# Heads of the first phase: queries and keys written from PSUM into the attention's operand tiles, without the way through DRAM

## The chip, the cores and the metric

The kernel runs on one core of a Trainium2 chip. The metric is the device time of one execution in microseconds (us). Three runs of the kernel before took 1397.95, 1398.54 and 1400.02 us; their median, 1398.54 us, is the time before. The profile is of one further execution. Its engines are PE (TensorE's matmuls; PEld is its weight loads), DVE (VectorE), ACT (ScalarE), POOL (GpSimd) and SP, whose queue issues nearly all DMAs.

## The reference

One layer of a hybrid encoder, run on 1024 prompt frames and on 32 sample frames of a running stream. The part that matters here is the input projection and the forgetting attention ("fox", 8 heads of 64) of the prompt:

```python
h = x * (1 + sc1) + sh1                      # x: 1056 x 1024 in all, sc1/sh1 from the conditioning vector
mq, mk, mv, mo, mi, mf, fq, fk, fv, ff, gu, gv = split(h @ w_in)
logf = log_sigmoid(ff + b_fox_f)             # a forget value for each frame and head
Ft = cumsum(logf)                            # over the frames
# in blocks of 128 queries:
logits = q @ k.T * 64 ** -0.5 + F[query] - F[key], masked causally
out = softmax(logits) @ v
```

Beside it stand an mLSTM (4 heads, with its own gates `mi`, `mf` and a running maximum over the frames), a gated spatial unit, the output projection with a norm, and a SwiGLU feed-forward with a norm. The keys `fk` are also an output of their own.

## The kernel before, in words

**Tiles and phases.** The frames are cut in two groups: group 0 is frames 0 to 511, group 1 is frames 512 to 1023 and the 32 sample frames. A float32 product is made as three matmuls on split operands (high by high, high by low, low by high; `gemm`, L111). The modulated input lies in SBUF as `h1h` and `h1l`. `fm_unit` (L236) makes 128 output columns of the projection: it loads and splits the weights (`weights`, L94: ACT writes the high part, DVE or POOL the low part), then runs one gemm for each range of frames, of 256 frames in group 0 and 272 in group 1, each into a PSUM bank of pool `pg`, which has three. `tm_unit` (L272) does the same with the frames on the partitions.

The first phase works on group 0. The string `ORDER` (L42) is its list of work: `q0` to `q7` are the units of fox head 0 to 7 (64 columns of queries and 64 of keys in one unit), `f0` to `f7` the attention of each head over the first 512 frames, `k0`, `k1`, `v`, `o` the mLSTM's projections, `m0` to `m3` its chunks, `a` a piece of the conditioning. Heads 0 and 1 (`QD`) run their group 1 ranges in the same unit; the other heads' come later.

**A head's way to its operands.** For each range `evac_qk` (L359) writes the high part `qkh` (ACT, L366, with the scale 0.125 on the query rows), the low part `qkl` (DVE, L367) and their sum `qkr` (POOL, L368), and stores them to DRAM: `dqh`, `dql`, and the output `o_kT`. `fox` (L672) then loads nine pieces into five tiles: `qp` (queries high over low), `k1` (keys high, twice), `q2` (queries high and four rows of forget terms), `k2` (keys low and four rows), `v`. `fox_chunk` (L699) makes the scores with two matmuls for each block of 128 queries (L717, L718), the mask, maximum, exponential and sum, the transposes of the probabilities (L753) and the product with `v` (L761 to L770).

**The gates.** `gates` (L387) comes ahead of `ORDER`. From the 16 gate columns it makes, mostly on DVE and on few partitions, the forget sums, which it stores as `dfs` in eight pieces (L434 to L442, tile `gates_fr` with two buffers), the running maximum of the mLSTM (`gates_cm`, seven doubling steps on DVE at L454 with small copies on POOL at L455), the values `gates_rs` (L484 to L487), and nine PE transposes of these (L492) into `col`. Its tiles lie in a pool of their own that is closed at the end of the function. The pool `mx0` (L1316), from which the operand tiles of fox and the tiles of the mLSTM come, is opened after that, and takes up the space again; a tile there waits until what lay in its place has been used.

**What sets the order.** A planner arranges the instructions of each engine when the kernel is built, by its own estimate of when each is ready; attention and mLSTM carry a higher priority (`HPA`, L1341). On the chip each engine, and SP's queue, then works through its list strictly in that order.

Of the kernel before, what the change touches and what calls it, by code (L numbers as in the profile page):

```python
# [7 lines left out]
F32 = mybir.dt.float32  # L8
F32R = mybir.dt.float32r
AF = mybir.ActivationFunctionType  # L10
ALU = mybir.AluOpType
# [54 lines left out]
def f(ap):  # L66
    return ap.bitcast(F32)


class Kernel:  # L70
# [288 lines left out]
    def evac_qk(self, h):  # L359
        nc = self.nc  # L360

        def evac(o, n, ps):
            hi = self.t(self.sm, [P, 272], F32R, "qkh", 3)
            lo = self.t(self.sm, [P, 272], F32R, "qkl", 2)
            kr = self.t(self.sm, [P, 272], F32, "qkr", 3)
            nc.scalar.activation(hi[:, :n], ps, AF.Copy, scale=self.qsc)  # L366
            nc.vector.scalar_tensor_tensor(lo[:, :n], ps, self.qsc, f(hi[:, :n]), ALU.mult, ALU.subtract)  # L367
            nc.gpsimd.tensor_tensor(kr[:, :n], f(hi[:, :n]), f(lo[:, :n]), ALU.add)  # L368
            self.store(self.dqh[h, :, o:o + n], f(hi[:, :n]))
            self.store(self.dql[h, :, o:o + n], f(lo[:, :n]))  # L370
            self.store(self.d["o_kT"][h, :, o:o + n], kr[64:, :n])
            if o + n == T:
                nc.gpsimd.tensor_copy(self.qks[:, h, :], kr[:, n - NS:n])
        return evac

    def evac_mqk(self, i, scale):
        nc = self.nc

        def evac(o, n, ps):
            r = self.t(self.sm, [P, 272], F32, "qkr", 3)  # L380
            nc.scalar.activation(r[:, :n], ps, AF.Copy, scale=scale)
            self.store(self.dmqk[:, i, o:o + n], r[:, :n])
        return evac
# [288 lines left out]
    def fox(self, h, chunks):  # L672
        self.phase = "fox"
        mx = self.mx
        q0, q1 = chunks[0][0] * P, (chunks[-1][-1] + 1) * P
        nq, nk, nb = q1 - q0, q1, q1 // P
        t = lambda shape, dt, tag, bufs: self.t(mx, shape, dt, tag, bufs)
        b = self.foxbufs
        k1 = t([P, nk], F32R, "k1", b[0])
        qp = t([P, nq], F32R, "qp", b[1])  # L680
        k2 = t([68, nk], F32R, "k2", b[2])
        q2 = t([68, nq], F32R, "q2", b[1])
        v = t([P, nb, P], F32R, "v", b[3])
        qs = slice(q0, q1)
        self.load(f(qp[0:64]), self.dqh[h, 0:64, qs])
        self.load(f(qp[64:128]), self.dql[h, 0:64, qs])
        self.load(f(k1[0:64]), self.dqh[h, 64:128, :nk])
        self.load(f(k1[64:128]), self.dqh[h, 64:128, :nk])
        self.load(f(q2[0:64]), self.dqh[h, 0:64, qs])
        self.load(f(q2[64:68]), self.dfs[h, 2:6, qs])  # L690
        self.load(f(k2[0:64]), self.dql[h, 64:128, :nk])
        self.load(f(k2[64:68]), self.dfs[h, 0:4, :nk])
        self.load(f(v), self.dv[:, :nb, h * P:(h + 1) * P])
        for tiles in chunks:
            o = tiles[0] * P - q0
            n = len(tiles) * P
            yield from self.fox_chunk(h, tiles, nk, n, k1, k2, qp[:, o:o + n], q2[:, o:o + n], v)

    def fox_chunk(self, h, tiles, W, nq, k1, k2, qp, q2, v):  # L699
        nc, mx = self.nc, self.mx  # L700
        nb = tiles[-1] + 1
        t = lambda shape, dt, tag, bufs: self.t(mx, shape, dt, tag, bufs)
        b5 = self.foxbufs[4]
        probs = []
        for i in tiles:
            n = (i + 1) * P
            qc = slice((i - tiles[0]) * P, (i - tiles[0] + 1) * P)
            half = n if n <= 512 else (n // 2 + 127) // 128 * 128
            cuts = [(0, half)] + ([(half, n)] if half < n else [])
            mxs = self.t(mx, [P, 2], F32, "fmx", 3)  # L710
            sums = self.t(mx, [P, 2], F32, "fsm", 3)
            pr = t([P, W], F32, "p", 4)
            banks = []
            for x, (lo, hi) in enumerate(cuts):
                s = self.t(self.pss, [P, 512], F32, "s")
                w = hi - lo
                nc.tensor.matmul(s[:, :w], qp[:, qc], k1[:, lo:hi], start=True, stop=False)  # L717
                nc.tensor.matmul(s[:, :w], q2[:, qc], k2[:, lo:hi], start=False, stop=True)  # L718
                if hi == n:
                    nc.vector.tensor_tensor(s[:, w - P:w], s[:, w - P:w], self.maskneg, ALU.add)  # L720
                nc.vector.tensor_reduce(mxs[:, x:x + 1], s[:, :w], AX.X, ALU.max, negate=True)
                banks.append(s)
            if len(cuts) > 1:
                nc.vector.tensor_tensor(mxs[:, 0:1], mxs[:, 0:1], mxs[:, 1:2], ALU.min)  # L724
            for x, (lo, hi) in enumerate(cuts):
                nc.scalar.activation(pr[:, lo:hi], banks[x][:, :hi - lo], AF.Exp, bias=mxs[:, 0:1],  # L726
                                     accum_out=sums[:, x:x + 1])
            if len(cuts) > 1:
                nc.vector.tensor_tensor(sums[:, 0:1], sums[:, 0:1], sums[:, 1:2], ALU.add)
            nc.vector.reciprocal(sums[:, 0:1], sums[:, 0:1])  # L730
            if FP[tiles[0] // 4]:
                nc.scalar.activation(pr[:, :n], pr[:, :n], AF.Copy, scale=sums[:, 0:1])
            else:
                nc.vector.tensor_scalar(pr[:, :n], pr[:, :n], sums[:, 0:1], None, ALU.mult)
            probs.append(pr)
            yield
            self.phase = "fox"


        o = self.t(self.po, [P, 512], F32, "o")  # L740
        full = tiles[0] + 1
        order = [0] + list(range(full, nb)) + list(range(1, full))
        units = [order[x:x + 2] for x in range(0, nb, 2)] if full > 1 else [[0], [1], [2, 3]]
        held = None
        for unit in units:
            ps = self.t(self.pt, [P, 512], F32, "t")
            at, e = [], 0
            for b in unit:
                first = max(0, b - tiles[0])
                w = nq - first * P  # L750
                for y in range(first, len(tiles)):
                    c = e + (y - first) * P
                    nc.tensor.transpose(ps[:, c:c + P], probs[y][:, b * P:(b + 1) * P], self.ident)  # L753
                at.append((b, slice(e, e + w), slice(first * P, nq)))
                e += w
            ph = t([P, 512], F32R, "pth", b5)
            pl = t([P, 512], F32R, "ptl", 2)
            nc.scalar.copy(ph[:, :e], ps[:, :e])
            nc.vector.tensor_tensor(pl[:, :e], ps[:, :e], f(ph[:, :e]), ALU.subtract)
            for b, c, q in at:  # L760
                nc.tensor.matmul(o[:, q] if b == 0 else o[0:64, q], v[:, b, :] if b == 0 else v[:, b, 0:64],  # L761
                                 pl[:, c], start=b == 0, stop=False)
                if b == 0 and full == 1:
                    held = ph
                else:
                    nc.tensor.matmul(o[:, q], v[:, b, :], ph[:, c], start=False, stop=full > 1 and b == order[-1])
            yield
            self.phase = "fox"
        if held is not None:
            nc.tensor.matmul(o[:, :nq], v[:, 0, :], held[:, :nq], start=False, stop=True)  # L770
        tmp = t([64, nq], F32, "fo", 1)
        r = t([64, nq], F32, "fr", 1)
        nc.scalar.copy(tmp[:, :nq], o[64:128, :nq])
        nc.vector.tensor_tensor(r[:, :nq], o[0:64, :nq], tmp[:, :nq], ALU.add)
        c = tiles[0] // 4
        o = tiles[0] * P - GO[c]
        self.store(self.dmix[c][64 * (h % 2):64 * (h % 2) + 64, 2 + h // 2, o:o + nq], r[:, :nq])
# [467 lines left out]
    def run(self):  # L1245
# [68 lines left out]
        more(T1[3])  # L1314
        s2 = ExitStack()
        self.mx = self.pool("mx0", ctx=s2)  # L1316
        self.foxbufs = (2, 1, 1, 2, 3)

        def emit(x):
            eng = nc.gpsimd if x[-1] == "p" else nc.vector  # L1320
# [4 lines left out]
            if x[0] == "m":  # L1325
                return self.mlstm(i)
            if x[0] == "q":
                self.fm_unit(w3[2 + i], self.evac_qk(i), (0, 1) if i < QD else (0,), eng)
            elif x[0] == "k":
                self.fm_unit(w3[i], self.evac_mqk(2 + i, 0.125), eng=eng)  # L1330
            elif x[0] == "s":
                self.mlstm_states()
            elif x[0] == "a":
                more(1)
            else:
                self.tm_unit(w2["-vo".index(x)], 256, self.evac_raw((None, self.dmv, self.dmo)["-vo".index(x)]), eng=eng)
# [251 lines left out]
```

## Time and profile before

| | |
|---|---|
| median of three runs | 1398.54 us |
| the profiled execution | 1397.36 us, of which its span is 1395.6 us |
| PE busy | 1346.8 us (97% of the span) |
| DVE busy | 1034.0 us (74%) |
| ACT busy | 641.6 us (46%) |
| POOL busy | 258.7 us (19%) |
| mean granted clock of PE | 0.988 |

The page shows first the busy time of each engine, then the span in 40 slices of 34.9 us with the busy share of each engine in tenths, the clock that TensorE was granted (PEclk) and the share of the DMA engines. In an answer of the timeline a row has its start in us, its duration, the engine (SPq is SP's queue), the source line, the operation with its output and input tiles, how many follow each other, and in brackets how long the engine had been idle before it and what released it. A row of stretches has the bounds in us, the length, the busy time of each engine with the number of instructions, the clock, and the DMA engines' share and rate. A row of waits has who waited for whom, the total, the number of times and the longest.

### The profile page before, as it was taken

What the parts mean: (1) busy time and instruction counts of PE and PEld (TensorE: products, weight loads), DVE (VectorE), ACT (ScalarE), POOL (GpSimd) and SP (SyncE); (2) the same over time, 40 slices, a digit from 0 to 9 for tenths busy, and PEclk for the clock granted to TensorE, in tenths of its full rate; (3) what the DMA queues carried; (4) which work ended last, traced back from release to release, by engine and by line L of the source; (5) the groups of instructions that cost most, each with busy time, mean ns of one, the idle gap of its engine ahead of it and who ended that gap; (6) DMA issues with size and microseconds to landing.
All of it is one profiled execution on the core that took longest, in us unless ns stands there. A gap on an engine that the chain in (4) does not pass through costs nothing.

```text
span 1395.6 us, 25879 instructions
## 1 busy us (share of the span) xinstructions
PE 1346.8 (97%) x9651; PEld 1238.7 (89%) x9651; DVE 1034.0 (74%) x2198; ACT 641.6 (46%) x1257; POOL 258.7 (19%) x292
## 2 busy tenths in 40 slices
PE   7999999999979799999999999999999999999996
PEld 4899988899979778888887889899999999999996
DVE  5548646678779657777776766678997988888777
ACT  3313234445445444545544445344673544545355
POOL 0103200052146500000000000264620000000341
PEclk9999999999999899999999999999999999999998
DMA  9764577585755656444443342555597767563321
GB/s 360 255 219 134 171 234 210 176 253 168 225 174 158 186 174 178 128 131 138 137 131 85 100 119 83 198 153 139 157 237 202 204 174 199 149 174 112 101 91 65
DMA packets 134709, 233.09 MB, mean 167 GB/s; under 512 B 22436, under 2 KB 77356, under 8 KB 134584
## 3 DMA queue, kind: packets, MB, share of 16 engines
q1 hardware_dynamic: 129272, 221.34, 51.3%
q0 software_dynamic: 5168, 9.96, 4.6%
q8 instruction: 76, 1.25, 0.4%
q14 instruction: 49, 0.40, 0.1%
q10 hardware_dynamic: 144, 0.14, 0.0%
HBM read 197.50 MB, written 53.81 MB: 180 GB/s over the span
## 4 chain that ended last, share of the span: by engine, by line
PE 68%; DVE 4%; DMA 3%; issue 1%; ACT 1%; SPq 0%; POOL 0%; DVEq 0%; ACTq 0%
PE up_g L117 5%; PE up_g L118 5%; PE up_g L119 5%; PE dn_g L119 4%; PE dn_g L117 4%; PE dn_g L118 4%; PE sup_u L119 3%; PE sup_u L117 3%; PE sup_u L118 3%; PE wo_g L117 2%; PE wo_g L118 2%; PE wo_g L119 2%; PE sup_g L118 2%; PE sup_g L119 2%; PE sup_g L117 2%; PE fox_t L753 2%
## 5 line engine op out<-in xcount | busy, mean ns | idle before, releaser
L117 PE MATMUL up_g<-mlstm_ah,up_whi 128*128 128x512 f32 (+1 forms) x384 | 142.4, 371 | 4.3 <-ACT lna_tmp L996 3.4
L118 PE MATMUL up_g<-mlstm_al,up_whi 128*128 128x512 f32 (+1 forms) x384 | 142.8, 372 | 0.6 <-DVE mlstm_al L1001 0.6
L119 PE MATMUL up_g<-mlstm_ah,up_wlo 128*128 128x512 f32 (+1 forms) x384 | 142.2, 371 | 0.0
L284 PE MATMUL tm_g<-tm_whi,start_h1l 128*128 128x256 f32 (+1 forms) x384 | 110.0, 287 | 0.0
L282 PE MATMUL tm_g<-tm_whi,start_h1h 128*128 128x256 f32 (+1 forms) x384 | 109.6, 287 | 0.0
L283 PE MATMUL tm_g<-tm_wlo,start_h1h 128*128 128x256 f32 (+1 forms) x384 | 109.5, 286 | 0.0
L117 PE MATMUL fm_g<-start_h1h,fm_whi 128*128 128x256 f32 (+2 forms) x344 | 101.9, 301 | 4.7 <-DVE fm_qkl L367 2.0
L118 PE MATMUL fm_g<-start_h1l,fm_whi 128*128 128x256 f32 (+2 forms) x344 | 101.6, 295 | 0.2 <-DVE start_h1l L223 0.2
L119 PE MATMUL fm_g<-start_h1h,fm_wlo 128*128 128x256 f32 (+2 forms) x344 | 100.8, 294 | 0.0
L1120 ACT CAST sup_whi<-sup_raw 128x1024 fp32r<-128x1024 f32 x54 | 56.0, 1048 | 90.3 <-PE dn_u L118 46.7
L117 PEld LDWEIGHTS up_g<-mlstm_ah,up_whi 128*128 128x128 f32 x384 | 74.2, 193 | 16.6 <-ACT mlstm_ah L1000 3.5
L118 PEld LDWEIGHTS up_g<-mlstm_al,up_whi 128*128 128x128 f32 x384 | 74.3, 193 | 12.6 <-DVE up_actl L1054 0.8
L119 PEld LDWEIGHTS up_g<-mlstm_ah,up_wlo 128*128 128x128 f32 x384 | 74.4, 194 | 10.7
L105 ACT CAST up_whi<-up_raw 128x1024 fp32r<-128x1024 f32 x50 | 52.4, 1049 | 62.0 <-PE dn_g L118 22.5
L726 ACT ACTIVATE fox_p<-fox_s,fox_fmx 128x384 f32<-128x384 f32 (+2 forms) x96 | 55.1, 579 | 50.6 <-DVE fox_fmx L724 43.9
L1121 DVE TENSOR_TENSOR sup_wlo<-sup_raw,sup_whi 128x1024 fp32r<-128x1024 f32 x54 | 68.1, 1265 | 10.5 <-ACT sup_whi L1120 10.5
L117 PEld LDWEIGHTS fm_g<-start_h1h,fm_whi 128*128 128x128 f32 x344 | 65.4, 192 | 10.3 <-issue 2.9
L282 PEld LDWEIGHTS tm_g<-tm_whi,start_h1h 128*128 128x128 f32 x384 | 72.3, 189 | 1.9 <-issue 1.2
L106 DVE TENSOR_TENSOR up_wlo<-up_raw,up_whi 128x1024 fp32r<-128x1024 f32 x50 | 67.1, 1341 | 9.2 <-ACT up_whi L105 8.5
L284 PEld LDWEIGHTS tm_g<-tm_whi,start_h1l 128*128 128x128 f32 x384 | 72.3, 188 | 1.5 <-issue 1.2
L117 PE MATMUL dn_g<-up_acth,dn_whi 128*128 128x512 f32 (+2 forms) x200 | 73.5, 368 | 0.0
L118 PE MATMUL dn_g<-up_actl,dn_whi 128*128 128x512 f32 (+2 forms) x200 | 73.3, 368 | 0.0
(591 smaller groups left out, 4592.9 us busy)
## 6 DMA issues: line engine op xcount, KB each, us to landing
up_raw<-w_gu SPq DMA_DIRECT2D x50, 512.0 KB
dn_raw<-w_dn SPq DMA_DIRECT2D x28, 512.0 KB
ada_late<-w_ada SPq DMA_DIRECT2D x24, 512.0 KB
wo_raw<-w_o SPq DMA_DIRECT2D x24, 512.0 KB
sup_raw<-w_gu SPq DMA_DIRECT2D x20, 512.0 KB
start_dp<-w_gu SPq DMA_DIRECT2D x19, 512.0 KB
start_dp<-w_gu POOLq DMA_DIRECT2D x19, 512.0 KB, 7.9
sup_raw<-start_dp SPq DMA_DIRECT2D x18, 512.0 KB
```

Of the source, the lines that this page charges most:

```text
L105: nc.scalar.copy(hi[:, :w], raw[:, :w])
L106: (eng or nc.vector).tensor_tensor(lo[:, :w], raw[:, :w], f(hi[:, :w]), ALU.subtract)
L117: nc.tensor.matmul(ps, hi, xh(k), start=start and k == 0, stop=False)
L118: nc.tensor.matmul(ps, hi, xl(k), start=False, stop=False)
L119: nc.tensor.matmul(ps, lo, xh(k), start=False, stop=stop and k == n - 1)
L282: nc.tensor.matmul(ps[:, :ncol], xh, hi, start=k == 0, stop=False)
L283: nc.tensor.matmul(ps[:, :ncol], xh, lo, start=False, stop=False)
L284: nc.tensor.matmul(ps[:, :ncol], xl, hi, start=False, stop=k == 7)
L726: nc.scalar.activation(pr[:, lo:hi], banks[x][:, :hi - lo], AF.Exp, bias=mxs[:, 0:1], accum_out=sums[:, x:x + 1])
L753: nc.tensor.transpose(ps[:, c:c + P], probs[y][:, b * P:(b + 1) * P], self.ident)
L1120: nc.scalar.copy(h, x)
L1121: tt(l, x, f(h), ALU.subtract)
```

## The change

Only the units `q0` to `q7` and what they use are changed. `head_unit` takes the place of `fm_unit` with `evac_qk` for group 0: it takes the head's five operand tiles at once, loads the forget rows and `v` into them, runs one gemm of 512 frames, and writes the queries and keys from PSUM straight into `qp`, `k1`, `k2` and `q2` with four ACT and two DVE instructions of 64 rows by 512. The keys' output goes through two ACT copies of 64 by 256; the high and low keys are still stored to `dqh` and `dql`, since the second half of the attention reads them, while the queries of group 0 are not. `fox` uses the tiles of `head_unit` where there are any. The operand tiles `qp`, `q2` and `k2` get two buffers where they had one (`foxbufs`). `qkh` and `qkr` get two buffers where they had three. At the end of a chunk the tile `fr` is gone: the sum is written into `fo` in place.

```diff
+    def head_tiles(self, h, nq, nk):
+        b = self.foxbufs
+        t = lambda shape, tag, bufs: self.t(self.mx, shape, F32R, tag, bufs)
+        return (t([P, nk], "k1", b[0]), t([68, nk], "k2", b[2]), t([P, nq], "qp", b[1]), t([68, nq], "q2", b[1]),
+                t([P, nk // P, P], "v", b[3]))
+
+    def head_unit(self, h):
+
+        nc = self.nc
+        w = self.weights(self.d["w_in_f"][2 + h], KT, P)
+        self.phase = "head"
+        k1, k2, qp, q2, v = self.heads[h] = self.head_tiles(h, 512, 512)
+        self.load(f(q2[64:68]), self.dfs[h, 2:6, :512])
+        self.load(f(k2[64:68]), self.dfs[h, 0:4, :512])
+        self.load(f(v), self.dv[:, :4, h * P:(h + 1) * P])
+        ps = self.t(self.pg, [P, 512], F32, "g")
+        self.gemm(ps, w, slice(0, P), *self.h1parts(0, 512))
+        lo, hi = slice(0, 64), slice(64, 128)
+        nc.scalar.activation(qp[lo], ps[lo], AF.Copy, scale=0.125)
+        nc.vector.scalar_tensor_tensor(qp[hi], ps[lo], 0.125, f(qp[lo]), ALU.mult, ALU.subtract)
+        nc.scalar.copy(k1[hi], ps[hi])
+        nc.vector.tensor_tensor(k2[lo], ps[hi], f(k1[hi]), ALU.subtract)
+        nc.scalar.copy(k1[lo], ps[hi])
+        nc.scalar.activation(q2[lo], ps[lo], AF.Copy, scale=0.125)
+        for o in (0, 256):
+            kr = self.t(self.sm, [P, 272], F32, "qkr", 2)
+            nc.scalar.copy(kr[hi, :256], ps[hi, o:o + 256])
+            self.store(self.d["o_kT"][h, :, o:o + 256], kr[hi, :256])
+        self.store(self.dqh[h, hi, :512], f(k1[hi]))
+        self.store(self.dql[h, hi, :512], f(k2[lo]))
+        if h < QD:
+            evac = self.evac_qk(h)
+            self.phase = "fm"
+            for o, n in self.ranges((1,)):
+                ps = self.t(self.pg, [P, 512], F32, "g")
+                self.gemm(ps[:, :n], w, slice(0, P), *self.h1parts(o, n))
+                evac(o, n, ps[:, :n])
...
     def evac_qk(self, h):
...
-            hi = self.t(self.sm, [P, 272], F32R, "qkh", 3)
+            hi = self.t(self.sm, [P, 272], F32R, "qkh", 2)
...
-            kr = self.t(self.sm, [P, 272], F32, "qkr", 3)
+            kr = self.t(self.sm, [P, 272], F32, "qkr", 2)
...
     def fox(self, h, chunks):
...
+        if h in self.heads:
+            k1, k2, qp, q2, v = self.heads.pop(h)
+        else:
+            k1, k2, qp, q2, v = self.head_tiles(h, nq, nk)
...
     def fox_chunk(...):
...
-        tmp = t([64, nq], F32, "fo", 1)
-        r = t([64, nq], F32, "fr", 1)
-        nc.scalar.copy(tmp[:, :nq], o[64:128, :nq])
-        nc.vector.tensor_tensor(r[:, :nq], o[0:64, :nq], tmp[:, :nq], ALU.add)
+        r = t([64, nq], F32, "fo", 1)
+        nc.scalar.copy(r[:, :nq], o[64:128, :nq])
+        nc.vector.tensor_tensor(r[:, :nq], o[0:64, :nq], r[:, :nq], ALU.add)
...
-        self.foxbufs = (2, 1, 1, 2, 3)
+        self.foxbufs = (2, 2, 2, 2, 3)
+        self.heads = {}
...
-                self.fm_unit(w3[2 + i], self.evac_qk(i), (0, 1) if i < QD else (0,), eng)
+                self.head_unit(i)
```

Over the kernel the built lists change by: PE 192 matmuls of 256 columns fewer in net (384 of 256 become 192 of 512); DVE the same number; ACT 32 more; POOL 16 fewer; SP 64 DMAs fewer. From the output projection of group 0 on, PE's list is the same in both.

More of the change, by code (lines that the diff above doesn't have):

```diff
@@ L379, in evac @@
         def evac(o, n, ps):
-            r = self.t(self.sm, [P, 272], F32, "qkr", 3)
+            r = self.t(self.sm, [P, 272], F32, "qkr", 2)
             nc.scalar.activation(r[:, :n], ps, AF.Copy, scale=scale)
@@ L676, in fox @@
         nq, nk, nb = q1 - q0, q1, q1 // P
[L677 to L693, printed above, removed]
+        if h in self.heads:
+            k1, k2, qp, q2, v = self.heads.pop(h)
+        else:
+            k1, k2, qp, q2, v = self.head_tiles(h, nq, nk)
+            qs = slice(q0, q1)
+            self.load(f(qp[0:64]), self.dqh[h, 0:64, qs])
+            self.load(f(qp[64:128]), self.dql[h, 0:64, qs])
+            self.load(f(k1[0:64]), self.dqh[h, 64:128, :nk])
+            self.load(f(k1[64:128]), self.dqh[h, 64:128, :nk])
+            self.load(f(q2[0:64]), self.dqh[h, 0:64, qs])
+            self.load(f(q2[64:68]), self.dfs[h, 2:6, qs])
+            self.load(f(k2[0:64]), self.dql[h, 64:128, :nk])
+            self.load(f(k2[64:68]), self.dfs[h, 0:4, :nk])
+            self.load(f(v), self.dv[:, :nb, h * P:(h + 1) * P])
         for tiles in chunks:
```

## The prediction

> **What bounds the kernel now.** I read the page's busy times and slices first.
>
> ```profile
> PE 1346.8 (97%) x9651; PEld 1238.7 (89%) x9651; DVE 1034.0 (74%) x2198; ACT 641.6 (46%) x1257; POOL 258.7 (19%) x292
> ...
> PE   7999999999979799999999999999999999999996
> ```
>
> PE is busy 97% of the span, and in the slices that hold the heads of the first phase (4 to 11, 34.9 us each) it stands at 9 tenths throughout. So a change gains only what PE waits, and loses whatever new time PE has to wait. Next come the stretches of that phase (bounds, length, busy time of PE, PEld, DVE, ACT, POOL with counts, clock, DMA).
>
> ```profile
> 122.00:148.00 26.00, 24.03 (x188) 23.83 (x187) 25.20 (x48) 8.26 (x19) 15.29 (x21) 0.93 0.35 100
> 146.00:363.00 217.00, 210.59 (x1747) 195.28 (x1746) 144.57 (x432) 88.52 (x222) 39.06 (x46) 1.00 0.67 200
> 141.00:147.00 6.00, 6.00 (x39) 6.00 (x40) 5.84 (x9) 2.40 (x5) 5.07 (x7) 0.72 0.30 78
> 391.00:395.00 4.00, 3.59 (x18) 3.60 (x18) 2.09 (x6) 1.91 (x5) 0.00 (x0) 0.53 0.26 70
> ```
>
> Between 146 and 363 us PE is idle for 217.0 - 210.6 = 6.4 us in all: that is everything that the rest of the phase can give back. Between 122 and 148 us DVE is the fullest engine, 25.2 of 26 us: it works off the gates there. The waits of PE in 140 to 320 us show what the change aims at:
>
> ```profile
> PE fm_g L117 <- DVE fm_qkl L367: 2.0, 1, 2.0
> ...
> PE fox_s L717 <- DMA fox_qp<-start_dql: 1.7, 1, 1.7
> PE fox_s L717 <- DMA fox_k<-start_dqh: 1.0, 1, 1.0
> ...
> PE fox_s L718 <- DMA fox_k<-start_dql: 0.5, 1, 0.5
> ```
>
> The attention's operands that come through DRAM cost PE 1.7 + 1.0 + 0.5 = 3.2 us; the DVE wait of 2.0 us is the evacuation of a head's unit queued behind the gates. Last I read the timeline where the gates end:
>
> ```profile
> 156.39 1.35 DVE L487 TENSOR_TENSOR gates_rs<-gates_rb,gates_me 4x1152 f32<-4x1152 f32 x1
> 160.22 1.03 PE L492 MATMUL gates_t<-start_ident,gates_rs 128*128 128x128 f32 x8
> 160.92 0.47 SPq L87 DMA_DIRECT2D fox_qp<-start_dqh  x1
> 163.82 0.53 POOL L525 MEMSET mlstm_mqb<- 128x512 f32 x1 [15.68 <-PE gates_t L492]
> ```
>
> The last value of `gates_rs` is written at 156.39 + 1.35 = 157.74 us, PE transposes it from 160.22 us, and only then does the first fox load go out (160.92) and the first mLSTM tile get cleared, after POOL waited 15.68 us for those transposes. So nothing from the pool `mx0` may be touched before the gates are through: it lies where their tiles lie. That costs PE nothing now. The head units' own tiles (`qkh`, `qkl`, `qkr`) are in another pool, and PE goes on with q0, q1, q2, k0, k1 from 106 to 160 us.
>
> **The change: where the new wait is.** `head_unit` writes from PSUM into `mx0` tiles. In the changed kernel's list the first ACT instruction of head 0 waits for the DVE instruction that writes the last `gates_rs` (the analogue of L487), and head 1's follows it. PE's list reads: q0 (24 matmuls of 512, then 48 of 272), q1 (24 of 512, with the first gates matmuls after 14 of them, then 24 of 272), the nine transposes of `gates_rs`, one conditioning piece, the scores of f0 for two blocks, and only then the last 24 of 272 of q1 (it needs the bank of head 0), then q2, k0 and k1. There PE was free to run q2, k0, k1 before; now all of that stands behind the gates in a list that goes strictly in order, and the three banks are then held by head 0, head 1 and the piece of q1 behind it in any case. When does PE get there?
>
> ```profile
> 130.15 0.49 ACT L366 ACTIVATE fm_qkh<-fm_g,start_qsc 128x272 fp32r<-128x272 f32 x1 [2.35 <-PE fm_g L119]
> 154.17 0.28 PE L117 MATMUL fm_g<-start_h1h,fm_whi 128*128 128x256 f32 x1
> 154.52 0.28 PE L117 MATMUL fm_g<-start_h1h,fm_whi 128*128 128x256 f32 x1
> 600.22 0.40 PE L117 MATMUL up_g<-mlstm_ah,up_whi 128*128 128x512 f32 x1
> 600.92 0.40 PE L117 MATMUL up_g<-mlstm_ah,up_whi 128*128 128x512 f32 x1
> ```
>
> ACT takes the first 272-wide piece of q1 from PE at 130.15 us, the last thing ahead of the wait. One step of three matmuls takes 154.52 - 154.17 = 0.35 us at 256 columns and 600.92 - 600.22 = 0.70 us at 512, so a head's 48 narrow ones (16 steps, 5.6 us) and 24 wide ones (8 steps, 5.6 us) cost the same: I put 0 for the 192 matmuls fewer, and the hole begins at 130.1 us.
>
> When does it end? The gates' DVE chain runs from the first `gates_rb` to 157.74 us:
>
> ```profile
> 121.41 0.58 ACT L428 COPY gates_rb<-gates_t 96x512 f32<-96x512 f32 x1 [2.56 <-PE gates_t L427]
> 123.56 1.71 SPq L91 DMA_DIRECT2D start_dfs<-gates_fr  x2
> 125.99 0.29 ACT L438 CAST gates_fr<-gates_ft 8x128 fp32r<-8x128 f32 x1 [0.96 <-DMA start_dfs<-gates_fr]
> 136.29 2.44 POOL L106 TENSOR_TENSOR fm_wlo<-fm_raw,fm_whi 128x1024 fp32r<-128x1024 f32 x1
> 136.41 2.48 DVE L440 TENSOR_SCALAR gates_fr<-gates_fr 8x256 fp32r<-8x256 f32 x1
> 143.83 1.10 DVE L440 TENSOR_SCALAR gates_fr<-gates_fr 8x256 fp32r<-8x256 f32 x1
> 145.63 1.21 DVE L106 TENSOR_TENSOR fm_wlo<-fm_raw,fm_whi 128x1024 fp32r<-128x1024 f32 x1
> 147.58 0.71 DVE L440 TENSOR_SCALAR gates_fr<-gates_fr 8x256 fp32r<-8x256 f32 x1
> L367 DVE SCALAR_TENSOR_TENSOR fm_qkl<-fm_g,start_qsc,fm_qkh x32: 466/484/501, 109.2 to 471.6; 128x256 fp32r<-128x256 f32 x16, 128x272 fp32r<-128x272 f32 x16
> ```
>
> What leaves this stretch of DVE's list: six evacuations (L367, 0.48 each, 2.9 us), one weight split (1.2), and the stretch of three copies L440 beside POOL work that goes (2.48 + 1.10 + 0.71 against 0.28 each, 3.4): 7.5 us. Against it the first `gates_rb` comes later, since 14 wide matmuls (3.3 us) stand ahead where 18 narrow ones (2.1) stood: 1.2 us. If DVE stays full, the chain ends at 157.74 - 7.5 + 1.2 = 151.4. It won't quite: `gates_fr` has two buffers, and from a store's issue (123.56) to the cast that reuses the buffer (125.99) there are 2.4 us, over three more rounds now with little between; I give 2.6 us of idle DVE. If nothing is gained it ends at 157.7 + 1.2 = 158.9. I take 154.0, nearer to the lower end, because DVE was 97% busy there. Part one: 154.0 - 130.1 = 23.9 us.
>
> [...]
>
> After that, head 0 must be evacuated before PE can go on:
>
> ```profile
> 156.21 0.15 DVE L479 TENSOR_TENSOR gates_d<-gates_m0x,gates_me 4x9 f32<-4x9 f32 x1
> 163.69 0.22 ACT L513 ACTIVATE fm_d0c<-fm_d0c 128x18 f32<-128x18 f32 x1 [3.21 <-DMA fm_d0c<-start_dd]
> 163.93 1.07 PE L179 MATMUL ada_t<-ada_late,start_c 128*32 128x256 f32 x16
> 164.38 0.28 ACT L495 ACTIVATE start_col<-start_col 128x108 f32<-128x108 f32 x1
> 165.07 0.37 ACT L182 COPY ada_adas<-ada_t 128x256 f32<-128x256 f32 x1 [0.40 <-PE ada_t L179]
> L773 ACT COPY fox_fo<-fox_o x24: 369/370/587, 195.8 to 882.5; 64x256 f32<-64x256 f32 x16, 64x512 f32<-64x512 f32 x8
> L381 ACT ACTIVATE fm_qkr<-fm_g x8: 384/388/398, 145.4 to 169.1; 128x256 f32<-128x256 f32 x4, 128x272 f32<-128x272 f32 x4
> L774 DVE TENSOR_TENSOR fox_fr<-fox_o,fox_fo x24: 406/417/683, 196.4 to 882.9; 64x256 f32<-64x256 f32 x16, 64x512 f32<-64x512 f32 x8
> ```
>
> ACT's list there holds the first query copies of both heads, then the exponential of `fm_d0c`, whose loads come from DRAM: it started 163.69 - 156.21 = 7.5 us after the DVE instruction that makes the value, which is 1.5 us ahead of the end of `gates_rs`; so 6.0 us after that end. Behind it: itself 0.22, L495 0.28, four copies of 64 by 512 (L773's 0.58, its maximum, for that shape), one conditioning copy 0.37, two key copies (L381's 0.39): 4.0 us. The bank is free 10.0 us after the gates. DVE's two low parts (L774's 0.68 each for such a shape) lie beside it. In these 10 us PE does nine transposes (1.0), the conditioning (1.1 and 0.2), four of the next piece (0.3) and four score matmuls (0.4): 3.0 us. Part two: 7.0 us idle; if the load of `fm_d0c` is there in time, the rest is two more copies (1.2) and the 4.0, so 2.2 idle.
>
> **The rest of the parts.** Restart: after a hole of 5 us ahead of 391 us the clock was 0.53 over 4 us, 1.9 us lost; I take that once (0 to twice, 3.8). Taken back: the 2.0 us DVE wait, and the clock of 0.72 over the 6 us after it (1.7), together 3.7. The fox waits on DRAM, 3.2; between nothing and all 6.4 us of PE's idle time. The eight attentions' nine loads become three, six stores four; SP has 64 fewer, at some 0.5 us each (the load at 160.92 took 0.47), which lies beside PE: 0. ACT does per head six copies and scaled copies of 0.58 and 0.39 in place of two: some 2.1 us more, 17 in all; it is busy 88.5 of 217 us, so 0. DVE +0.4 a head, POOL 1.5 less: 0. Two buffers of `qkh` and `qkr` in place of three, and `fo` in place: a copy now waits for the store two before it, in SP's order, and in ACT's list an attention's exponential can stand behind that copy. No row shows it; nothing to 1 us a head over six heads, 0 to 6, and I take 0 because PE has two other banks, a 24-matmul tile each of 2.8 us. If that cover is gone, the 6 us apply. From the output projection on, PE's list is unchanged: 0.
>
> Sum: 23.9 + 7.0 + 1.9 - 3.7 - 3.2 = +25.9 us on the profiled execution's 1397.36 (span 1395.6): 1423.3. The median of the runs, 1398.54, lies 1.2 us above it: **1424**.
>
> [...]
>
> **Rivals.** *A shorter hole* (chance 0.19): DVE full to the end (151.4), the `fm_d0c` load in time (2.2 idle), no slow restart, all 6.4 us given back: 21.3 + 2.2 - 3.7 - 6.4 = +13.4, some 1412. For it: DVE's 97%. Against: the 3.21 us that ACT waited for that load. *A longer one* (0.20): the chain as slow as now (158.9), the clock lost twice, 6 us of new store waits behind two buffers, nothing given back: 28.8 + 7.0 + 3.8 + 6 - 3.7 = +42, some 1440; halfway, about 1435. For it: POOL's small copies and clears stand in one list and wait for stores. *The other side: the head units aren't held* (0.03). If the gates were through by the time PE arrives, the change would give its 3.2 and the 3.7 back: 1398.5 - 6.9 = 1392, faster. It decides if PE's wait stays under 6.9 us, so if the operands are ready by about 137 + 3 = 140 us; the gates' chain from 121.4 us would have to shrink from 36 us to under 9, and DVE alone is 25 us busy in it. *No change* (0.02): a hole of just that size.
>
> **How the numbers follow.** The forecast (0.56) holds 1416 to 1432 with the bounds taken singly. Both its neighbours are slower too, so slower by over 0.2% (2.8 us, about what a measurement of this kernel tells from none) has 0.56 + 0.19 + 0.20 = 0.95; faster 0.03, same 0.02. The range for 8 in 10 goes from the short hole, 1410, into the long one, 1437.
>
> **What would show it.** Right: a hole of PE of over 20 us from about 130 us, ended by the gates' last DVE value, a second one ended by ACT's copies of head 0, PE's slice 4 at 7 tenths and slice 5 at 3 or 4, fewer SP rows, no wait of a score matmul on a DRAM load before 363 us, the stages after 363 us shifted by some 25 us as a whole. Wrong: PE running matmuls of q2 or k0 between 130 and 150 us; the chain of gates ending before 145 us; or holes in f0 to f7 of more than 10 us together, which would put the loss on buffers and not on the gates.

## The result, and the profile after

The changed kernel takes 1420.21 us (median of 4 runs, 1418.96 to 1425.81) against 1399.28 us of the kernel before on the same chip (4 runs, 1397.95 to 1400.02; three of them are those of the time before): a ratio of 1.0156, with a 95% interval of 1.0136 to 1.0176. The ratios here are worked out over the single runs; the quotient of the two medians is 1.0150. It is slower, by 20.9 us between the medians. The profiled execution took 1418.96 us, with a span of 1417.0 us.

The page of the changed kernel, busy times and three rows of slices (35.4 us each):

```profile
PE 1344.6 (95%) x9459; PEld 1227.8 (87%) x9459; DVE 1033.9 (73%) x2198; ACT 657.4 (46%) x1289; POOL 242.2 (17%) x276
...
PE   7996599998989989999999999999999999999996
...
PEclk9999699999999999999999999999999999999998
```

PE does no more work than before (1344.6 us against 1346.8), but slices 4 and 5 fell from 9 tenths to 6 and 5, and the clock in slice 5 to 6 tenths. The waits of PE between 129 and 200 us in the changed kernel (line, releaser, us in total, times, longest):

```profile
PE gates_t L530 <- DVE gates_rs L525: 23.6, 1, 23.6
PE ada_t L185 <- ACT ada_adas L182: 1.7, 1, 1.7
PE ada_t L179 <- DMA ada_late<-w_ada: 1.5, 1, 1.5
PE fm_g L117 <- ACT head_qkr L402: 1.1, 1, 1.1
PE fox_s L752 <- ACT head_k L398: 0.5, 1, 0.5
```

The first row is the hole. The timeline of the changed kernel around its end (start us, us, engine, line, operation, in brackets the idle time before it and what ended it; the rows of DVE, ACT and PE are each from their own engine's list):

```profile
151.80 1.35 DVE L525 TENSOR_TENSOR gates_rs<-gates_rb,gates_me 4x1152 f32<-4x1152 f32 x1
...
153.19 1.07 ACT L394 ACTIVATE head_qp<-head_g 64x512 fp32r<-64x512 f32 x2 [14.11 <-DVE gates_rs L525]
157.78 0.22 ACT L551 ACTIVATE fm_d0c<-fm_d0c 128x18 f32<-128x18 f32 x1 [3.52 <-DMA fm_d0c<-start_dd]
161.04 0.64 ACT L402 COPY head_qkr<-head_g 64x256 f32<-64x256 f32 x2
...
153.30 2.15 PE L530 MATMUL gates_t<-start_ident,gates_rs 128*128 128x128 f32 x9 [23.58 <-DVE gates_rs L525]
163.33 1.08 PE L179 MATMUL ada_t<-ada_late,start_c 128*32 128x256 f32 x8 [1.46 <-DMA ada_late<-w_ada]
164.73 0.43 PE L118 MATMUL fm_g<-start_h1l,fox_whi 128*128 128x272 f32 x1
169.22 0.28 PE L117 MATMUL fm_g<-start_h1h,fox_whi 128*128 128x272 f32 x1
```

The gates' last value is there at 151.80 + 1.35 = 153.15 us. ACT's first copies of head 0 and head 1 start 0.04 us later, PE's transposes 0.15 us later. Then ACT stands 3.52 us for `fm_d0c`, and head 0's bank is free at 161.68 us. A matmul of 272 columns takes 0.43 us there and 0.28 us from 169.2 us on: until then PE ran at half its clock (0.50 granted from 153.3 to 169.2 us).

To see where the time came from, I cut both traces at the place where the output projection goes on after its own wait (391.4 us before, 418.2 us after). The rows have bounds, length, busy time of PE, PEld, DVE, ACT, POOL, clock and DMA. The kernel before:

```profile
129.70:391.40 261.70, 247.83 (x2037) 231.61 (x2035) 175.54 (x484) 106.18 (x259) 53.31 (x66) 0.99 0.67 201
391.40:1383.60 992.20, 979.26 (x6673) 903.95 (x6674) 774.64 (x1478) 491.14 (x907) 190.35 (x194) 0.99 0.52 148
```

and the changed kernel:

```profile
129.70:418.20 288.50, 249.10 (x1891) 226.24 (x1890) 180.79 (x487) 123.83 (x295) 42.87 (x57) 0.94 0.52 158
418.20:1405.00 986.80, 975.79 (x6673) 900.58 (x6674) 773.47 (x1478) 491.17 (x907) 189.96 (x194) 0.99 0.53 148
```

Up to the cut the changed kernel loses 288.5 - 261.7 = 26.8 us. Nearly all of it is idle PE: 39.4 us against 13.9, so 25.5 us more. PE's busy time is only 1.3 us longer. Behind the cut, where PE's list is the same in both, it is 5.4 us shorter.

### The profile page after: what moved, and what is told of

Same layout as the page of the kernel before. It is cut to its first block, busy times and chain, and to the rows that moved or that the text cites. A ratio compares the mean times of both kernels' runs of the same rounds, so it can differ in the third digit from the quotient of the medians.

```text
span 1417.0 us, 25445 instructions
## 1 busy us (share of the span) xinstructions
PE 1344.6 (95%) x9459; PEld 1227.8 (87%) x9459; DVE 1033.9 (73%) x2198; ACT 657.4 (46%) x1289; POOL 242.2 (17%) x276
## 4 chain that ended last, share of the span: by engine, by line
PE 79%; DVE 9%; DMA 5%; ACT 3%; issue 2%; SPq 1%; POOL 1%; DVEq 0%; ACTq 0%; POOLq 0%
PE up_g L117 5%; PE up_g L118 5%; PE up_g L119 5%; PE dn_g L119 4%; PE dn_g L117 4%; PE dn_g L118 4%; PE sup_u L119 3%; PE sup_u L117 3%; PE sup_u L118 3%; PE tm_g L283 2%; PE tm_g L282 2%; PE tm_g L284 2%; PE wo_g L117 2%; PE wo_g L118 2%; PE fox_t L788 2%; PE wo_g L119 2%
## 5 line engine op out<-in xcount | busy, mean ns | idle before, releaser
L105 ACT CAST up_whi<-up_raw 128x1024 fp32r<-128x1024 f32 x50 | 52.5, 1049 | 62.6 <-PE dn_g L118 20.9
L283 PEld LDWEIGHTS tm_g<-tm_wlo,start_h1h 128*128 128x128 f32 x384 | 72.2, 188 | 2.6 <-issue 1.2
L119 PE MATMUL dn_g<-up_acth,dn_wlo 128*128 128x512 f32 (+2 forms) x200 | 73.3, 366 | 0.0
L105 ACT CAST dn_whi<-dn_raw 128x1024 fp32r<-128x1024 f32 (+1 forms) x44 | 42.7, 971 | 49.7 <-PE dn_u L118 11.6
L793 ACT CAST fox_pth<-fox_t 128x512 fp32r<-128x512 f32 (+1 forms) x80 | 41.2, 544 | 51.5 <-PE fox_t L788 51.2
```

Of the source, the lines that this page charges most:

```text
L105: nc.scalar.copy(hi[:, :w], raw[:, :w])
L119: nc.tensor.matmul(ps, lo, xh(k), start=False, stop=stop and k == n - 1)
L283: nc.tensor.matmul(ps[:, :ncol], xh, lo, start=False, stop=False)
```

## The experiments

Theory: heads 0 and 1 write their operands into tiles that lie in the gates' space, so their PSUM banks stay full until the gates are through, and PE has nothing else that it could do. Rivals: the cost is in the head units' own work (six ACT copies a head, fewer buffers, new stores), or in the order of the units. The kernel before took 1394.15, 1393.59 and 1393.31 us in the three groups of runs below, so runs are compared by their ratios to it.

**The operand tiles in a pool of their own, and k0, k1 ahead of q2.** (Tiles of the first phase alone; the later phase uses its own pool for both.)

```
+        s2 = ExitStack()
+        self.mh = self.pool("mh0", ctx=s2)      # k1, k2, qp, q2
         self.gates()
         more(T1[3])
-        s2 = ExitStack()
         self.mx = self.pool("mx0", ctx=s2)      # all the rest, v too
...
-ORDER = "q0 f0 q1 a f1 a q2 f2 k0 k1p s a q3 ..."
+ORDER = "q0 f0 q1 a f1 a k0 k1p q2 f2 s a q3 ..."
```

> The changed kernel with two edits: the heads' k1, k2, qp and q2 tiles get a pool of their own that is opened ahead of the gates (v stays in mx0 and is loaded at the attention's start), and the two key units of the mLSTM stand ahead of q2 in the order. Theory (the gates' space holds the heads): heads 0 and 1 are evacuated at once, PE goes on with the rest of q1 and k0, k1 until the gates end, and the wait of 23.6 us on gates_rs is under 3 us; time 1392 to 1402. Rival (the cost is in the head units' own work: six ACT copies a head, fewer buffers, stores): the time stays above 1412, wherever the tiles lie.

Measured: 1390.21 us, ratio 0.9963 (0.9944 to 0.9982). PE's waits from 100 to 420 us, the largest:

```profile
PE fm_g L117 <- DVE fm_qkl L367: 4.5, 2, 2.9
PE fm_g L117 <- ACT fm_qkr L418: 3.0, 1, 3.0
```

No wait on `gates_rs` is left, and the same direct way from PSUM is now faster than the kernel before. The work of the head units is not what cost, nor are its matmuls of 512 columns, which this kernel has too. But two things were changed at once.

**The new order alone, in the changed kernel.** The second half of the edit above.

> The changed kernel with the new order alone (k0 and k1 ahead of q2), tiles as in the changed kernel. Theory: heads 0 and 1 are still held, and k0 and k1 stand behind them in PE's list, so the wait on gates_rs stays at 22 to 25 us and the time at 1416 to 1424. Rival (the order is what fills the hole): the time falls to about 1400, as with the pool of its own.

Measured: 1418.01 us, ratio 1.0176 (1.0136 to 1.0217), and the wait on `gates_rs` is that of the changed kernel:

```profile
PE gates_t L530 <- DVE gates_rs L525: 23.5, 1, 23.5
```

This order without the space does nothing.

**The pool alone, in the changed kernel's order.** The first half of the edit.

> The changed kernel with the pool of its own for k1, k2, qp and q2, in the changed kernel's order. Theory: heads 0 and 1 are evacuated at once, but q2 stands next in PE's list and needs the tiles of head 0, which f0 can't release before the gates are through; with two pieces of k0 behind it all three banks are held again. PE has 24 matmuls of 512 columns more to do and 48 of about 264 (11 us) than in the changed kernel, so the wait on gates_rs is about 12 us in place of 23.6, and the time about 1.008 times that of the kernel before. Rival (the space alone was the matter): no wait of over 4 us there, and a ratio of 0.996 as with the new order.

Measured: 1409.88 us, ratio 1.0110 (1.0089 to 1.0131). The wait, of this kernel:

```profile
PE gates_t L529 <- DVE gates_rs L524: 12.3, 1, 12.3
```

The hole shrinks to what the work of q1 and q2 leaves of it, 12.3 us against the 12 worked out. The time is longer than the 1.008 worked out, since the clock and the waits behind the hole weren't in it: PE was at half clock from 159.3 to about 163 and from 169.3 to 176.6 us (0.67 granted from 160 to 170 us, 0.66 from 170 to 180), and between the two it waited another 3.0 us for a conditioning load. So the space alone is not enough; there must also be work behind the heads that needs neither the gates nor the heads before. (Whether the space can be done without is tried further below, with k0 and k1 ahead of q0.)

**The place alone, in the kernel before.** The old way through DRAM; only the high parts of heads 0 and 1 are moved into `mx0`.

```
-            hi = self.t(self.sm, [P, 272], F32R, "qkh", 3)
+            first = h < QD and o < 512
+            hi = (self.t(self.mx, [P, 272], F32R, "qkh0", 2) if first
+                  else self.t(self.sm, [P, 272], F32R, "qkh", 3))
```

> The kernel before, through DRAM as it was; only the high parts (qkh) of heads 0 and 1 for the first group lie in mx0, so in the gates' space. Theory: the place alone makes the hole. PE's list has three pieces of q0, then the gates' matmuls and their transposes: PE stops about 118 us and the gates end about 152, so a hole of 30 to 36 us and a time of 1425 to 1438. Rival (the place does nothing, the direct evacuation does): no new wait, 1396 to 1402.

Measured: 1418.65 us, ratio 1.0172 (1.0138 to 1.0206), as slow as the whole change:

```profile
PE gates_t L493 <- DVE gates_rs L488: 26.1, 1, 26.1
...
144.97 2.15 PE L493 MATMUL gates_t<-start_ident,gates_rs 128*128 128x128 f32 x9 [26.06 <-DVE gates_rs L488]
```

The place of these tiles makes the hole without any of the rest. I had expected it 30 to 36 us long, but the gates were through at 145 us and not at 152; with PE stopped DVE had fewer evacuations between them.

**The changed kernel with heads 0 and 1 through DRAM.**

```
-                self.head_unit(i)
+                if i < 2:
+                    self.fm_unit(w3[2 + i], self.evac_qk(i), (0, 1) if i < QD else (0,), eng)
+                else:
+                    self.head_unit(i)
```

> The changed kernel, but heads 0 and 1 go through DRAM as before; from head 2 on the direct way. Theory: nothing is held until q2, whose 24 matmuls come after q0 and q1, and then two pieces of k0, about 133 to 140 us; the gates end near 157 us as in the kernel before, so a hole of 10 to 17 us: a ratio of 1.005 to 1.010. Rival (it is only heads 0 and 1 that cost): 0.998 to 1.001.

Measured: 1414.22 us, ratio 1.0145 (1.0122 to 1.0167). The hole is 12.5 us, as expected, but the cost is more than the 1.005 to 1.010 expected. The stretches behind it show why (the column ahead of the last two is the clock):

```profile
150.00:160.00 10.00, 1.22 (x6) 1.25 (x7) 7.99 (x27) 0.00 (x0) 0.00 (x0) 0.54 0.10 35
160.00:170.00 10.00, 6.55 (x31) 3.56 (x29) 3.65 (x17) 1.57 (x7) 0.00 (x0) 0.50 0.67 195
170.00:180.00 10.00, 9.31 (x40) 5.44 (x39) 7.39 (x23) 6.49 (x18) 0.00 (x0) 0.50 0.95 272
180.00:184.00 4.00, 4.00 (x25) 3.83 (x25) 0.88 (x3) 0.55 (x2) 0.00 (x0) 0.82 0.24 78
```

Behind the hole PE worked in short pieces with waits of 0.5 to 1.2 us between them, and the clock stayed at half for over 20 us, from the end of the hole at 158.8 to about 181 us. Each stretch's busy time by one minus its clock gives 0.6 + 3.3 + 4.7 + 0.7 = 9.3 us, lost beside the hole.

**The load of `fm_d0c` out of the way of head 0's copies.** The exponential is put behind head 1's last key copy on ACT.

```
...
-        nc.scalar.activation(self.d0c, self.d0c, AF.Exp)
+        with self.tc.issue_after(self.kr1.ins):     # head 1's last copy of keys
+            nc.scalar.activation(self.d0c, self.d0c, AF.Exp)
```

> The changed kernel with the exponential of fm_d0c put behind the last key copy of head 1 in ACT's list. It tests the second hole by itself. Theory: ACT no longer stands 3.5 us for that load, head 0's copies end 3 to 3.7 us earlier, PE's waits behind the gates (on ada_adas and on the conditioning's load) shrink by that, and the time is 2 to 4 us below the changed kernel's: a ratio of 1.013 to 1.015 to the kernel before. Rival (another wait, the load of the next conditioning piece, ends the second hole anyway): under 1 us less, 1.015 to 1.017.

Measured: 1416.72 us, ratio 1.0163 (1.0129 to 1.0197): no gain that shows, though the intervals of the two ratios are too wide to exclude 2 us. The trace is clearer. In this kernel:

```profile
154.90 1.07 ACT L394 ACTIVATE head_qp<-head_g 64x512 fp32r<-64x512 f32 x2 [14.11 <-DVE gates_rs L527]
161.50 0.64 ACT L402 COPY head_qkr<-head_g 64x256 f32<-64x256 f32 x2
...
PE ada_t L179 <- DMA ada_late<-w_ada: 2.8, 1, 2.8
```

From the first copy to the last ACT takes 162.14 - 154.90 = 7.2 us, where it took 161.68 - 153.19 = 8.5 with the wait on the load. Of the 3.5 us only 1.3 came back, since other waits of ACT (1.4 and 0.4 us on DVE, 0.6 us on PE) took the place. And PE gave those back: its wait on the next conditioning load rose from 1.5 to 2.8 us. From the start of the transposes to q1's last piece PE takes 11.1 us (155.02 to 166.14), against 11.0 in the changed kernel (153.30 to 164.34). The rival was right.

**The small parts alone, in the kernel before.** Two buffers for `qkh` and `qkr`, and the sum in place.

```
-"qkh", 3  ...  "qkr", 3
+"qkh", 2  ...  "qkr", 2
...
-        nc.scalar.copy(tmp[:, :nq], o[64:128, :nq])
-        nc.vector.tensor_tensor(r[:, :nq], o[0:64, :nq], tmp[:, :nq], ALU.add)
+        nc.scalar.copy(r[:, :nq], o[64:128, :nq])
+        nc.vector.tensor_tensor(r[:, :nq], o[0:64, :nq], r[:, :nq], ALU.add)
```

> The kernel before with the small parts of the change alone: qkh and qkr with two buffers in place of three, and the attention's output summed in place. The prediction put 0 on them, with 0 to 6 us as bounds: 1397 to 1401. If the 5 us that the changed kernel took back between 418 us and its end came from the sum in place, this kernel is at 1392 to 1395.

Measured: 1393.60 us beside 1394.15, ratio 1.0002 (0.9983 to 1.0022). The absolute bounds of the expectation went by the first runs of the kernel before, 1399.28; beside the runs of this group it is no change, so these parts cost nothing and gave no 5 us either.

**The new order alone, in the kernel before.**

> The kernel before, through DRAM, with the new order alone (k0 and k1 ahead of q2). It tells what of the gain of the pool of its own with the new order (ratio 0.9963) is the order's. If the direct way gives the 3.2 us of the DRAM waits and the 2.0 of the wait on DVE, this kernel stays at 0.999 to 1.002; if the order made the gain, it is at 0.995 to 0.998.

Measured: 1396.50 us, ratio 1.0013 (0.9993 to 1.0032). This order gains nothing where the operands still go through DRAM.

**Matmuls of 512 columns alone, in the kernel before.** One matmul tile per head's first group, copied out in two pieces.

```
...
+                ps = self.t(self.pg, [P, 512], F32, "g")
+                self.gemm(ps, w, slice(0, P), *self.h1parts(0, 512))
+                evac(0, 256, ps[:, :256])
+                evac(256, 256, ps[:, 256:])
...
```

> The kernel before, with 24 matmuls of 512 columns in place of 48 of 256 for a head's first group, copied out in two pieces as before. The prediction put 0 on the widths; with the banks held longer a wait may come: ratio 0.998 to 1.003.

Measured: 1413.38 us, ratio 1.0133 (1.0100 to 1.0167), a clear miss. Waits of PE in this kernel, 100 to 420 us:

```profile
PE fm_g L117 <- DVE gates_cm L461: 6.1, 1, 6.1
...
PE tm_g L282 <- DVE tm_traw L352: 3.1, 1, 3.1
PE fox_o L761 <- DVE fox_ptl L759: 2.5, 1, 2.5
PE fox_t L753 <- DVE ada_adam L187: 2.3, 1, 2.3
```

A wide tile holds its bank until both pieces are copied, and DVE's part of that stands between the gates' instructions: PE waited 6.1 us for it at 147 to 153 us (DVE copied the two pieces at 150.1 and 152.9 us; the row names the instruction behind the second), and three more times for DVE later. At 1.0133 this is nearly the cost of the whole change, so it is a rival to the held tiles. It doesn't explain the change: the changed kernel's hole is ended by `gates_rs`, PE waits for nothing from 200 to 300 us there, and the kernels with a pool of their own have the wide tiles and are faster than the kernel before. There the heads are copied by other instructions, and what their wide tiles cost beside the gates this run can't tell.

**k0 and k1 ahead of q0, the tiles in the gates' space as in the change.**

> The changed kernel, tiles in the gates' space as they are, with k0 and k1 put ahead of q0 in the order. Theory: what costs is that PE has nothing to do that doesn't need the gates' space. Now 23 us of key units and q0's pieces stand ahead of the first held bank's next user, so PE reaches the transposes about 150 us, near the gates' end (152 to 157): a wait on gates_rs of 2 to 7 us, no second hole, ratio 0.996 to 1.002. Rival (the head units cost in themselves while they are held): 1.010 or more.

Measured: 1391.22 us, ratio 0.9984 (0.9964 to 1.0003), and PE has no wait on `gates_rs` left, where I had expected 2 to 7 us. The gates are through at 149.6 us there and PE comes to the transposes at 149.9. The hole can be filled as well as avoided, and in this order no space of its own was needed. This is the prediction's other side, the gates through by the time that PE arrives, made by an order.

**The pool of its own, with k0 and k1 in two other places.** `ORDER = "q0 f0 k0 q1 a f1 a k1p q2 ..."`, and `"k0 k1p q0 f0 q1 ..."`.

> The pool of its own, with k0 between q0 and q1 and k1 behind q1. The key pieces are evacuated by ACT alone, so fewer of PE's tiles wait for DVE beside the gates: the waits on fm_qkl and fm_qkr (4.5 and 3.0 us with k0 and k1 behind q1) should fall to 2 to 5 together and the ratio to 0.993 to 0.997. If DVE's list orders them as before, no change against 0.996.

> The pool of its own, with k0 and k1 ahead of q0. During the first part of the gates only ACT evacuates; the heads come near the gates' end. Waits on fm_qkl and fm_qkr 0 to 5 us; ratio 0.993 to 0.998. If the pool of its own adds nothing once the order is so, the same ratio as with this order alone.

Measured: 1384.11 us, ratio 0.9927 (0.9899 to 0.9955), with k0 between the heads, and 1387.22 us, 0.9947 (0.9926 to 0.9967), with both ahead. The first is just under the 0.993 to 0.997 expected. Its rows, from 100 to 420 us and in the stretch of the gates:

```profile
PE fm_g L117 <- DVE fm_qkl L367: 2.9, 1, 2.9
PE fm_g L117 <- DVE gates_me L504: 0.8, 1, 0.8
...
129.00:200.00 71.00, 69.84 (x509) 60.80 (x508) 52.80 (x140) 32.76 (x79) 6.21 (x14) 1.00 0.56 167
```

PE is idle for 1.2 us of these 71, where the changed kernel has 42.52 us of work in the same window. The waits on `fm_qkl` and `fm_qkr` fell from 7.5 to 2.9 us; a further 0.8 us is put down to a gates' instruction. It is the fastest of the kernels here, and beats both the kernel before and the changed one. Its interval overlaps that of the other order (0.9926 to 0.9967), so which of the two is better stays open.

## Why the prediction was right

It gave 1424 (1410 to 1437) and slower with 0.95; the time is 1420.21. Step by step:

- **Where the new wait is.** Right. The hole is ended by `gates_rs` L525, and the place of the tiles makes it: with the place alone it comes into the kernel before (26.1 us), with a pool of its own and other work in between it goes (ratio 0.9963). One reading was too broad, that nothing from `mx0` may be touched before the gates are through. In the changed kernel POOL clears an mLSTM tile of `mx0` 9.7 us before the gates' last value is there:

```profile
143.45 0.52 POOL L563 MEMSET mlstm_mqb<- 128x512 f32 x1
```

  So a tile waits for what lay in its own place, and the heads' tiles lay where `gates_rs` is still in use. Whether they could lie elsewhere in `mx0`, where the gates are done earlier, no run tried.
- **Part one, 23.9 us from 130.1 to 154.0.** Measured 23.6, from 129.7 to 153.3. The end of the gates came within 0.9 us of 154.0, partly by luck: three terms were each off by about 1 us, and not all the same way. From the first `gates_rb` to the last `gates_rs`, before and then after:

```profile
121.41:157.74 36.33, 34.36 (x273) 34.16 (x272) 34.16 (x80) 11.36 (x25) 15.63 (x22) 0.95 0.42 126
```

```profile
122.25:153.15 30.90, 7.47 (x54) 6.79 (x52) 25.34 (x73) 3.75 (x11) 6.01 (x15) 0.71 0.07 17
```

  DVE's busy time fell by 34.16 - 25.34 = 8.8 us (predicted 7.5), its idle time rose from 2.2 to 5.6 us, so by 3.4 (predicted 2.6), and the start came 0.8 us later (predicted 1.2). The 3.4 us for three long copies came as priced: they took 2.48, 1.10 and 0.71 us before (L440), and in the changed kernel all eight copies of this kind take 0.28 (L478). That POOL's work beside them made them long was my estimate from the rows; no run tried it alone.
- **Part two, 7.0 us idle, and restart, 1.9 us.** The sum is near, the split is not. PE was idle 3.8 us (nearly all of it in the waits of 1.7, 1.5 and 0.5) and lost some 6 us to the clock. For 153.3 to 165 us PE was busy 7.86 us at 0.50, so 3.9 us, and from 165 to 171 us 6.0 us at 0.65, so 2.1 us:

```profile
153.30:165.00 11.70, 7.86 (x42) 4.53 (x43) 6.04 (x19) 6.68 (x17) 0.00 (x0) 0.50 0.57 161
165.00:171.00 6.00, 6.00 (x35) 5.33 (x34) 1.56 (x4) 1.41 (x4) 1.71 (x3) 0.65 0.49 148
```

  That is 9.8 us in place of 8.9. (The slices stand at 6 and 5 tenths, where I had named 7 and 3 or 4.) The 3.0 us of PE's work inside the wait for ACT had been priced at full clock; it ran at half and so took the place of idle time. The restart, 1.9 with a bound of 3.8, was the mis-sized term. (By PE's busy time of 3.59 us in the row that it was read from, it would have been 1.7.) The wait was also named wrongly at its end: head 0's bank was free 8.5 us after the gates (predicted 10.0), but PE took up q1's last piece only at 164.3 us, behind a conditioning piece whose load came late. Moving the exponential of `fm_d0c` therefore gained nothing.
- **Taken back, 3.7, and the fox waits on DRAM, 3.2.** Right in sign and size: no score matmul waits for a load of the operands up to the cut, and 200 to 300 us has no wait. Three more waits of before went as well (1.7 on `mlstm_mo`, 0.9 and 0.6), 3.2 us, which makes the upper bound of 6.4; why they went wasn't traced. Against them stand new ones that I had at 0, 2.3 us on the mLSTM's `mlstm_mqk` load, 1.4 on `fox_ptl`, 1.1 on `head_qkr`, 0.9 on `tm_wlo` and 1.5 of small ones, together 7.2.
- **Widths, ACT, SP, buffers and the sum in place at 0.** The buffers and the sum are shown in the kernel before (1.0002); in the changed one PE's 1.1 us on `head_qkr` came at 187 us from ACT's list, where head 2's copies stood behind a mLSTM exponential that waited 3.57 us for DVE, and not from a store. ACT's copies are covered (0.9963 with all of them). For the widths, the matmuls themselves cost the same (three of 512 columns take 0.70 us in the changed kernel, three of 256 took 0.35 before), but that a wide tile holds its bank longer isn't nothing: 1.0133 in the kernel before.
- **The sum.** +25.9 was predicted and +26.8 measured up to the cut at the output projection. That these are so near is partly luck: the second part with its restart cost 0.9 us more than predicted and the new waits 7.2 us, while 3.2 us more of the old waits went, the wait at the cut itself shrank by 0.6, and PE had some 3 us less work than the terms give (busy time without what the clock took: 249.1 - 6.0 us after, 247.8 - 1.7 before), which no run here explains. Behind it the step "From the output projection on, PE's list is unchanged: 0" stood, and the profile has -5.4. The two rows of the same work, from the first LayerNorm sums on, before and then after:

```profile
436.00:1383.60 947.60, 936.65 (x6341) 862.04 (x6340) 735.27 (x1430) 468.56 (x872) 159.94 (x168) 0.99 0.52 147
```

```profile
462.70:1405.00 942.30, 933.23 (x6341) 858.62 (x6340) 733.77 (x1430) 468.68 (x872) 158.90 (x168) 1.00 0.52 147
```

  The kernel before with the small parts alone has 942.3 us for the same stage, the one with the held tiles 943.8, the one with the new order 945.6. So a single profile of this stage can't tell 5 us from nothing, and the profile of before that the sum was made against was the longest of them. What sets it apart is the clock in a few stretches (7.8 us lost to it, 3.4 in the changed kernel, added up by single microseconds) and waits of PE of 1 to 3 us (10.9 us idle, against 9.1); what decides these wasn't settled.
- **The rivals.** Shorter and longer holes didn't come. (Halfway from 1424 to 1440 is 1432, not the 1435 given.) The other side was worked out at 1392 us, a ratio of 1392 / 1398.5 = 0.995, if PE's wait stayed under 6.9 us: the three kernels whose wait does so by the pool of its own have 0.9963, 0.9947 and 0.9927, the one by order alone 0.9984. In us of 1393 to 1394 these are 5.2, 7.4, 10.2 and 2.2, around the 6.9 worked out; the last is not told from none by its interval (up to 1.0003). The order has its part in each, and how much of the gain is the direct way's alone no run separates.

## What to carry to other kernels

Here tiles placed in the space of a closed pool waited for the last use of what lay in their place, the evacuations from PSUM into them held the banks for as long, and PE stood 23.6 us: look where a new operand tile lies, not only how many buffers it has. A transfer through DRAM that looks like waste may be what lets an engine run ahead, as it did here (1399.28 us with it, 1420.21 without), so put the room and the work that can fill the time in place first, and cut the detour then. In these runs a hole in PE cost more than its length where the work behind it came in pieces: 12.5 us of hole cost 20 us of time (heads 0 and 1 through DRAM), while 26.1 us cost 24 (the held tiles, with 7.9 us of unbroken work behind, 144.97 to 152.88).

## What the runs showed of the hardware

The half clock lasted longer than I had allowed. Behind the 23.6 us hole a stretch of 16 us ran at half speed, 153.3 to 169.0 us (0.50 granted), while PE was busy for 67% of its first 11.7 us. Behind the 12.5 us hole of the kernel with heads 0 and 1 through DRAM it was over 20 us. The end of that hole and the last gap of over half a microsecond in its slow stretch:

```profile
158.78 2.15 PE L530 MATMUL gates_t<-start_ident,gates_rs 128*128 128x128 f32 x9 [12.54 <-DVE gates_rs L525]
...
175.51 0.76 PE L753 MATMUL fox_s<-fox_k,fox_q 68*128 68x128 f32 x2 [0.56 <-DMA head_k<-start_dfs]
```

In both kernels full clock came some 6 us after the last gap of over half a microsecond (163.3 and 175.5 us). In the kernel with the held tiles, PE had unbroken work behind its hole of 26.1 us, which ended at 144.97 us, and it was at full clock 4.3 us later:

```profile
149.25 0.29 PE L118 MATMUL fm_g<-start_h1l,fm_whi 128*128 128x272 f32 x1
```

So the half clock lasted 4.3 us behind a hole where PE's work had no gap, and 16 and over 20 us behind two where it had gaps of over half a microsecond. That the gaps kept the clock down is my estimate from these three; no run tried it alone, and gaps would not be the whole of it. In the kernel with the pool alone PE shows no gap behind a wait of 3.0 us, and yet full clock came only 7.3 us after it, at 176.6 us:

```profile
169.31 1.03 PE L179 MATMUL ada_t<-ada_late,start_c 128*32 128x256 f32 x2 [3.02 <-DMA ada_late<-w_ada]
...
176.60 0.35 PE L118 MATMUL fm_g<-start_h1l,fm_whi 128*128 128x272 f32 x1
176.79 0.29 PE L119 MATMUL fm_g<-start_h1h,fm_wlo 128*128 128x272 f32 x1
```

What held the clock back there stays open.
